# Longer links in the feed-forward chain, and the down projection's operand placed ahead of the convolution's tiles

## The chip, the cores and the metric

The kernel runs on one core of a Trainium2 chip. The metric is the device time of one execution in microseconds, given as a median of runs. The core has TensorE (PE, with its weight loads PEld), VectorE (DVE), ScalarE (ACT), GpSimd (POOL) and SyncE (SP, which issues most DMAs). Each engine works through its own list of instructions in order, and a semaphore holds an instruction back until what it needs is done.

## The reference

Two transformer blocks over 256 positions of width 2048, in float32. Each block has a mixer (attention in the first, a gated recurrence in the second) and then a feed-forward part with a convolution of width 3 over the positions. The change touches only the two feed-forward parts:

```python
# first block: causal convolution with a bias, gelu
u = causal_dwconv(h @ w_up[l], conv_w[l], conv_b[l])
gate, up = jnp.split(u, 2, axis=-1)
y = (jax.nn.gelu(gate, approximate=True) * up) @ w_down[l]
# second block: centred convolution without a bias, silu
up = dwconv3(h @ w_in, w_conv)
gate, val = jnp.split(up, 2, axis=-1)
return (jax.nn.silu(gate) * val) @ w_out
```

The inner width is 5632, so `h @ w_up` has 88 groups of 128 output features (44 of gate and 44 of up, taken alternately) and the down projection has 44 groups of 128 input features.

## The kernel before, in words

**Products.** Every float32 product is made of three: weights and activations are split into a high and a low half, and TensorE sums high by high, high by low and low by high. Weights come in *units* of 128x1024 numbers (512 KB): SP loads a unit (`ws`, L125), ACT writes its high half (`wh`, L143), DVE its low half (`wl`, L144). `Weights.ahead` splits a unit two units ahead of its use; three buffers each of `wh` and `wl` are there, so a split waits until TensorE has done with the unit three before it.

**Feed-forward stage.** The first eight groups of features are computed together (`wave`), in four PSUM banks, two groups to a bank. The other 80 are *blocks* (`block`): one group, one bank, two units, and for each unit eight matmuls of the high half (L359, 128x512) and eight of the low half (L364, 128x256). Then the down projection runs over the gated result (`v_chunk(ahl)`), four chunks of 512 columns.

**Chain.** For each group a *task* (a generator) does the work behind the product, with single instructions on ACT and DVE:

- for a block, `whole` copies half of the bank to `part` (ACT L374) and adds the other half to it (DVE L376); this add is what gives the block's bank back to TensorE
- `z` = that times the row factor R (DVE L1103); for a group of the wave this reads the bank itself and gives it back when both groups of the bank are through
- `u` = the convolution: one instruction on ACT (L1111, or L1113 in the second block), two on DVE (L1116)
- for a gate group `s` = gelu or silu of `u` (ACT L1128); for an up group `u` times `s` (DVE L1138), its high half `ah` (ACT L1141) and its low half `al` (DVE L1143), which are the down projection's operand

**What sets the order.** The kernel is recorded in the order in which Python runs, and each engine gets its instructions in that order. While matmuls are recorded, `bg.tick()` is called between them, and every fourth tick is one *step*: each waiting task runs on to its next `yield`. A unit of a block has eight ticks, so two steps; a block has four. A `yield` in a task puts what follows it one step later, and so behind whatever else is recorded meanwhile on that engine. A block's task starts when the block is recorded. The wave's eight tasks start 6 steps apart (`1 + 6 * i`).

**Banks.** There are four banks for products and two more are lent from those of the background. While the wave's tasks still hold their banks, the next block has to take the bank of a block that has just ended.

**Pools.** The tiles `z0` to `z2` (three, handed round in a list), `ah` and `al` come from one pool, placed in memory in the order of the code; `u` has four buffers and `s` two.

Of the kernel before, what the change touches and what calls it, by code (L numbers as in the profile page):

```python
# [11 lines left out]
F32 = mybir.dt.float32  # L12
F32R = mybir.dt.float32r
# [5 lines left out]
P = 128  # L19
T = 256  # L20
# [3 lines left out]
FB = DFF // P  # L24
# [146 lines left out]
def two_blocks(ctx: ExitStack, tc: tile.TileContext, a: dict, out: bass.AP, dbg=None):  # L171
    nc = tc.nc
    bg = Background()
# [39 lines left out]
    def evacuated(v):  # L213
        left = mm_use.pop(id(v))[1]
        left[0] -= 1
        if not left[0]:
            left[1].free += 1
            if left[1] is banks and lend[1]:
                lend[0] += 1
# [68 lines left out]
    def slot(name, shape=(P, KB, 2, T), dtype=F32R):  # L288
        return act_p.tile(list(shape), dtype, name=name, tag="pair")
# [60 lines left out]
    def block(src):  # L350


        ps, = mm_ps((0, 2 * T))
        for k0 in range(0, KB, 8):
            h, l = W.take()
            for j in range(8):
                k = k0 + j
                need(src, k)
                nc.tensor.matmul(ps, h[:, j, :], src.pair[:, k, :, :], start=k == 0, stop=False)  # L359
                if j % 3 < 2:  # L360
                    bg.tick()
            for j in range(8):
                k = k0 + j
                nc.tensor.matmul(ps[:, T:], l[:, j, :], src.hi[:, k, :], start=False, stop=k == KB - 1)  # L364
                if j % 4 == 3:
                    bg.tick()
        return ps

    def whole(ps):

        if ps.shape[-1] == T:
            return ps
        s = parts.tile([P, T], F32, name="part")
        nc.scalar.activation(s, ps[:, T:], AF.Copy)  # L374
        yield
        nc.vector.tensor_tensor(s, ps[:, :T], s, op=ALU.add)  # L376
        evacuated(ps)
        return s
# [317 lines left out]
    def out_chunks(src, name, yg, gb, g):  # L696

        pss = wave_t(src)
        back = Back(name, yg(), gb())
        for c in range(2):  # L700
            later(back.evac, c, pss[c])
        later(back.evac, 2, v_chunk(src, CH))
        ld = Lead(back, g)
        pss = v_chunk(src, CH, last=2, lead=ld)
        return ld, pss
# [4 lines left out]
    with first:  # L710
# [65 lines left out]
        fr, pss = boundary(None, None, G_PRE1, hhl, xT)  # L776
# [286 lines left out]
        for i in range(8):  # L1063
# [3 lines left out]
            if i in (1, 4, 5):  # L1067
# [7 lines left out]
        back, pss = out_chunks(mhl, "g_post1", lambda: ac.tile([P, 2, D], F32, name="yg", tag="bias"),  # L1075
                               lambda: slot("gb", (P, D), F32), G_PREF1)
        hp.close()
        hhl = Pair(slot("hhl"))
        fr, pss = boundary(back, pss, G_PREF1, hhl)
# [4 lines left out]
    def ffn(hhl, fr, pss, cw, cb, centred, post, g=None):  # L1084
        with ExitStack() as ph:
            fc = ph.enter_context(tc.tile_pool(name="fc", bufs=1))
            ft = ph.enter_context(tc.tile_pool(name="ft", bufs=4))
            z0 = 1 if centred else 2
            zs = [fc.tile([P, T + 32], F32, name=f"z{i}") for i in range(3)]
            for z in zs:  # L1090
                nc.vector.memset(z[:, 0:z0], 0.0)
                if centred:
                    nc.vector.memset(z[:, T + 1:T + 2], 0.0)
            ahl = Operand(fc.tile([P, FB, T], F32R, name="ah"), fc.tile([P, FB, T], F32R, name="al"))
            gated = {}
            lend[:] = 2, True

            def conv(i, ps):
                y = yield from whole(ps)
                while not zs:  # L1100
                    yield
                z = zs.pop()
                nc.vector.tensor_tensor(z[:, z0:z0 + T], y, fr.R, op=ALU.mult)  # L1103
                if y is ps:
                    evacuated(ps)
                yield
                yield
                yield
                u = ft.tile([P, T], F32, name="u")
                if cb is not None:  # L1110
                    nc.scalar.activation(u, z[:, 2:2 + T], AF.Identity, scale=cw[:, i, 2:3], bias=cb[:, i:i + 1])  # L1111
                else:
                    nc.scalar.activation(u, z[:, 2:2 + T], AF.Copy, scale=cw[:, i, 2:3])  # L1113
                yield
                for j in range(2):
                    nc.vector.scalar_tensor_tensor(u, z[:, j:j + T], cw[:, i, j:j + 1], u,  # L1116
                                                   op0=ALU.mult, op1=ALU.add)
                zs.append(z)
                return u

            def gate_task(i, ps, lag=1):
                for _ in range(lag):
                    yield
                u = yield from conv(i, ps)
                yield
                yield
                s = ft.tile([P, T], F32, name="s", bufs=2)
                nc.scalar.activation(s, u, AF.Silu if centred else AF.Gelu_apprx_tanh)  # L1128
                gated[i // 2] = s

            def up_task(i, ps, lag=1):
                for _ in range(lag):
                    yield
                u = yield from conv(i, ps)
                f = i // 2
                while f not in gated:
                    yield
                nc.vector.tensor_mul(u, gated.pop(f), u)  # L1138
                yield
                yield  # L1140
                nc.scalar.activation(ahl.hi[:, f, :], u, AF.Copy)  # L1141
                yield
                nc.vector.tensor_tensor(ahl.lo[:, f, :], u, ahl.hi[:, f, :], op=ALU.subtract)  # L1143
                ahl.ready.add(f)

            for i in range(WAVE):
                bg.add((up_task if i % 2 else gate_task)(i, pss[i], 1 + 6 * i))
            for i in range(WAVE, 2 * FB):
                bg.add((up_task if i % 2 else gate_task)(i, block(hhl)))
            back = Back(post, *yg_gb(slot("yg", (P, 3, D), F32)))  # L1150
            for c in range(3):
                later(back.evac, c, v_chunk(ahl, CH, FB))
            if g is None:
                pss = v_chunk(ahl, CH, FB, last=3)
                bg.flush()
            else:
                back = Lead(back, g)
                pss = v_chunk(ahl, CH, FB, last=2, lead=back)
            lend[:] = 0, False
        return back, pss  # L1160

    back, pss = ffn(hhl, fr, pss, convw, convb, False, "g_postf1", G_PRE2)

    with ExitStack() as ph:
# [4 lines left out]
        fr, pss = boundary(back, pss, G_PRE2, hhl)  # L1172
# [147 lines left out]
        back, pss = out_chunks(mhl, "g_post2", after_input, lambda: t[0][1], G_PREF2)  # L1320
        hp.close()
        hhl = Pair(slot("hhl"))
        fr, pss = boundary(back, pss, G_PREF2, hhl)

    back, pss = ffn(hhl, fr, pss, f2conv, None, True, "g_postf2")
# [110 lines left out]
```

## Time and profile before

| | |
|---|---|
| runs | 2578.93, 2579.96 and 2581.62 us, median 2579.96 us |
| profiled execution | 2579.38 us |
| its span, first to last instruction | 2577.6 us (1.8 us lie around it) |
| TensorE busy | 2547.7 us, 99% |
| TensorE's weight loads | 86% |
| DVE, ACT, POOL busy | 69%, 53%, 2% |
| granted TensorE clock | 0.999 |
| feed-forward stages in the trace | up projection 484 to 934 us and 1874 to 2324 us, each with 80 blocks behind its wave |

The profiled execution is the one in which the trace was taken; sums made from rows of the trace belong to its time. The span leaves out what lies before the first and behind the last instruction.

### The profile page before, as it was taken

Reading aid. Unit: us, or ns where it says so; the run is one execution under the profiler, and the core shown is the slowest. Engines: PE = TensorE matmul, PEld = TensorE weight load, DVE = VectorE, ACT = ScalarE, POOL = GpSimd, SP = SyncE. Lnnn points to the kernel's source line nnn. Section 1 sums busy time; section 2 is a strip of 40 time slices with the busy share of each in tenths; the row PEclk is TensorE's granted clock in tenths of the full one; section 3 lists DMA queues with packets and bytes.
Section 4 is the critical chain, followed back from the end, with each engine's and each line's share of the span. In section 5 each row is a group of like instructions: output and inputs, shape, how many; then the busy total and the mean of one; then the engine's idle time right before and its main releaser. Section 6 shows DMA issues by size and latency. Waiting matters only on the chain.

```text
span 2577.6 us, 38072 instructions
## 1 busy us (share of the span) xinstructions
PE 2547.7 (99%) x14400; PEld 2223.9 (86%) x14400; DVE 1771.3 (69%) x2967; ACT 1365.8 (53%) x2274; POOL 46.5 (2%) x66
## 2 busy tenths in 40 slices
PE   9999999999999999999999999999999999999998
PEld 9899988988888888889888888888988888888887
DVE  6666655687777764446777777785678877775444
ACT  5655554665555553445555555554565555554443
POOL 0000000000000000000000000000000000000000
PEclk9999999999999999999999999999999999999999
DMA  7854555556555565555544454546556555556554
GB/s 243 263 172 148 170 172 179 173 185 192 189 189 186 192 205 188 188 188 169 165 161 158 142 170 143 166 133 196 166 175 194 189 186 192 190 188 205 188 188 147
DMA packets 134229, 466.13 MB, mean 181 GB/s; under 512 B 15547, under 2 KB 20572, under 8 KB 133532
## 3 DMA queue, kind: packets, MB, share of 16 engines
q1 hardware_dynamic: 130572, 456.11, 54.9%
q10 hardware_dynamic: 2784, 2.92, 0.6%
q0 software_dynamic: 688, 4.65, 0.5%
q8 instruction: 113, 1.85, 0.3%
q14 instruction: 72, 0.59, 0.1%
HBM read 460.74 MB, written 2.88 MB: 180 GB/s over the span
## 4 chain that ended last, share of the span: by engine, by line
PE 93%; DVE 3%; ACT 2%; issue 1%; DMA 1%; POOL 0%; DVEq 0%; POOLq 0%; ACTq 0%; SPq 0%
PE mm L359 32%; PE mm L364 17%; PE mm L422 9%; PE mm L421 9%; PE mm L427 9%; PE mm L399 2%; PE mm L400 2%; PE mm L406 2%; PE bg L1248 2%; DVE wl L144 1%; ACT wh L143 1%; PE bg L421 1%; PE bg L422 1%; PE bg L427 1%; DMA ws<-in_cw 1%
## 5 line engine op out<-in xcount | busy, mean ns | idle before, releaser
L144 DVE TENSOR_TENSOR wl<-ws,wh 128x1024 fp32r<-128x1024 f32 (+1 forms) x865 | 1049.7, 1214 | 701.4 <-ACT wh L143 693.8
L143 ACT ACTIVATE wh<-ws 128x1024 fp32r<-128x1024 f32 (+1 forms) x865 | 906.5, 1049 | 743.4 <-PE mm L422 297.5
L359 PE MATMUL mm<-hhl,wh 128*128 128x512 f32 x3808 | 982.7, 396 | 3.5 <-ACT ah L1141 3.5
L359 PEld LDWEIGHTS mm<-hhl,wh 128*128 128x128 f32 x3808 | 679.3, 189 | 120.6 <-ACT ah L1141 3.8
L364 PEld LDWEIGHTS mm<-hhl,wl 128*128 128x128 f32 x3808 | 519.2, 190 | 38.1
L364 PE MATMUL mm<-hhl,wl 128*128 128x256 f32 x3808 | 530.6, 282 | 0.0
L422 PE MATMUL mm<-wh,al 128*128 128x512 f32 x684 | 269.9, 395 | 0.0
L421 PE MATMUL mm<-wh,ah 128*128 128x512 f32 x684 | 269.9, 395 | 0.0
L427 PE MATMUL mm<-wl,ah 128*128 128x512 f32 x684 | 186.7, 395 | 0.0
L427 PEld LDWEIGHTS mm<-wl,ah 128*128 128x128 f32 x684 | 128.9, 188 | 30.1
L422 PEld LDWEIGHTS mm<-wh,al 128*128 128x128 f32 x684 | 128.9, 188 | 30.0
L421 PEld LDWEIGHTS mm<-wh,ah 128*128 128x128 f32 x684 | 128.9, 188 | 30.0
L1228 ACT ACTIVATE kk<-lv 128x256 f32<-128x256 f32 x112 | 47.7, 435 | 118.1 <-DVE lv L1259 105.2
L399 PE MATMUL mm<-hhl,wh 128*128 128x256 f32 x398 | 104.8, 295 | 4.7 <-ACT wh L143 4.7
L400 PE MATMUL mm<-hhl,wh 128*128 128x256 f32 x398 | 101.0, 285 | 0.0
L376 DVE TENSOR_TENSOR part<-mm,part 128x256 f32<-128x256 f32 x238 | 99.3, 417 | 0.0
L374 ACT ACTIVATE part<-mm 128x256 f32<-128x256 f32 x238 | 87.2, 366 | 0.2
L1116 DVE SCALAR_TENSOR_TENSOR u<-z,c_convw,u 128x256 f32<-128x256 f32 x176 | 84.8, 482 | 3.1
L1116 DVE SCALAR_TENSOR_TENSOR u<-z,c_f2conv,u 128x256 f32<-128x256 f32 x176 | 84.8, 482 | 3.1
L399 PEld LDWEIGHTS mm<-hhl,wh 128*128 128x128 f32 x398 | 77.3, 194 | 5.3 <-ACT wh L143 4.7
L1248 PE MATMUL bg<-lv,kk 128*128 128x128 f32 x448 | 74.0, 288 | 5.8 <-ACT kk L1228 5.6
L1248 PEld LDWEIGHTS bg<-lv,kk 128*128 128x128 f32 x448 | 65.0, 191 | 16.1 <-ACT kk L1228 10.3
(380 smaller groups left out, 2638.0 us busy)
## 6 DMA issues: line engine op xcount, KB each, us to landing
ws<-in_wup SPq DMA_DIRECT2D x160, 512.0 KB, 3.9
ws<-in_f2in SPq DMA_DIRECT2D x160, 512.0 KB, 3.9
ws<-in_hin SPq DMA_DIRECT2D x112, 512.0 KB, 3.5
ws<-in_wdown SPq DMA_DIRECT2D x88, 512.0 KB, 3.4
ws<-in_f2out SPq DMA_DIRECT2D x88, 512.0 KB, 3.4
ws<-in_win_f SPq DMA_DIRECT2D x48, 512.0 KB, 4.0
ws<-in_hv SPq DMA_DIRECT2D x32, 512.0 KB, 3.4
ws<-in_win_vb SPq DMA_DIRECT2D x24, 384.0 KB, 3.2
```

Of the source, the lines that this page charges most:

```text
L143: self.nc.scalar.activation(h[:, c], src[:, c], AF.Copy)
L144: self.nc.vector.tensor_tensor(l[:, c], src[:, c], h[:, c], op=ALU.subtract)
L359: nc.tensor.matmul(ps, h[:, j, :], src.pair[:, k, :, :], start=k == 0, stop=False)
L364: nc.tensor.matmul(ps[:, T:], l[:, j, :], src.hi[:, k, :], start=False, stop=k == KB - 1)
L376: nc.vector.tensor_tensor(s, ps[:, :T], s, op=ALU.add)
L399: nc.tensor.matmul(pss[b], h[:, b, :], src.hi[:, k, :], start=first, stop=False, skip_group_check=True)
L400: nc.tensor.matmul(pss[b], h[:, b, :], src.lo[:, k, :], start=False, stop=False, skip_group_check=True)
L421: nc.tensor.matmul(ps, rows_of(src, k0 + j, t, 0), h[:, j, :], start=k0 + j == 0, stop=False)
L422: nc.tensor.matmul(ps, rows_of(src, k0 + j, t, 1), h[:, j, :], start=False, stop=False)
L427: nc.tensor.matmul(ps, rows_of(src, k0 + j, t, 0), l[:, j, :], start=False, stop=k0 + j == last)
L1116: nc.vector.scalar_tensor_tensor(u, z[:, j:j + T], cw[:, i, j:j + 1], u, op0=ALU.mult, op1=ALU.add)
L1248: nc.tensor.matmul(ps[:, t * P:(t + 1) * P], kk[:, t * P:(t + 1) * P], view(lv, T + t * P, [[2 * m, nb], [T + m, 2], [1, m]]), start=True, ...
```

## The change

Seven edits, all in the function `ffn`, which both blocks call:

1. `ahl` (the tiles `ah` and `al`) is allocated ahead of `z0` to `z2`, so the operand and the small tiles change places in memory.
2. In `conv`, three steps instead of one lie between the ACT part of the convolution and its DVE part.
3. In `gate_task`, three steps instead of two lie between the convolution and `s`.
4. `s` has three buffers instead of two.
5. In `up_task`, three steps instead of two lie between the product with `s` and `ah`.
6. In `up_task`, three steps instead of one lie between `ah` and `al`.
7. The wave's tasks start 10 steps apart instead of 6.

```diff
             z0 = 1 if centred else 2
+            ahl = Operand(fc.tile([P, FB, T], F32R, name="ah"), fc.tile([P, FB, T], F32R, name="al"))
             zs = [fc.tile([P, T + 32], F32, name=f"z{i}") for i in range(3)]
...
-            ahl = Operand(fc.tile([P, FB, T], F32R, name="ah"), fc.tile([P, FB, T], F32R, name="al"))
...
                     nc.scalar.activation(u, z[:, 2:2 + T], AF.Copy, scale=cw[:, i, 2:3])
                 yield
+                yield
+                yield
                 for j in range(2):
...
                 yield
                 yield
-                s = ft.tile([P, T], F32, name="s", bufs=2)
+                yield
+                s = ft.tile([P, T], F32, name="s", bufs=3)
...
                 yield
                 yield
+                yield
                 nc.scalar.activation(ahl.hi[:, f, :], u, AF.Copy)
+                yield
+                yield
                 yield
                 nc.vector.tensor_tensor(ahl.lo[:, f, :], u, ahl.hi[:, f, :], op=ALU.subtract)
...
-                bg.add((up_task if i % 2 else gate_task)(i, pss[i], 1 + 6 * i))
+                bg.add((up_task if i % 2 else gate_task)(i, pss[i], 1 + 10 * i))
```

**Place A: DVE, the fifth block of the first feed-forward stage, kernel before.** The rows are DVE's list, in order. `part<-mm` (L376) is the add that gives a block's bank back; `part_5291<-mm_5204` is that of the third block, and the fifth block's product `mm_5321` waits for it. `wl` are low halves of weights, `z1<-mm_4442` is a task of the wave.

```order
L144 TENSOR_TENSOR wl_5266<-ws_5205,wh_5265 128x1024
L1103 TENSOR_TENSOR z1_5095<-mm_4442,R_5083 128x256
L144 TENSOR_TENSOR wl_5296<-ws_5231,wh_5295 128x1024
L1143 TENSOR_TENSOR al_5101<-u_5242,ah_5100 128x256
L1116 SCALAR_TENSOR_TENSOR u_5289<-z2_5096,c_convw_120,u_5289 128x256 x2
L1138 TENSOR_TENSOR u_5289<-s_5274,u_5289 128x256
L376 TENSOR_TENSOR part_5291<-mm_5204,part_5291 128x256
```

The same stretch of DVE's list with the change, and on to the next block. Here `part_5282<-mm_5201` is the add of the third block, for which the fifth block's product `mm_5312` waits, and `part_5343<-mm_5255` that of the fourth, for which the sixth block's `mm_5370` waits.

```order
L144 TENSOR_TENSOR wl_5259<-ws_5202,wh_5258 128x1024
L1118 SCALAR_TENSOR_TENSOR u_5224<-z1_5097,c_convw_120,u_5224 128x256 x2
L144 TENSOR_TENSOR wl_5287<-ws_5228,wh_5286 128x1024
L376 TENSOR_TENSOR part_5282<-mm_5201,part_5282 128x256
L1103 TENSOR_TENSOR z1_5097<-part_5282,R_5083 128x256
L144 TENSOR_TENSOR wl_5316<-ws_5256,wh_5315 128x1024
L1118 SCALAR_TENSOR_TENSOR u_5280<-z2_5098,c_convw_120,u_5280 128x256 x2
L1141 TENSOR_TENSOR u_5280<-s_5310,u_5280 128x256
L1118 SCALAR_TENSOR_TENSOR u_5295<-z0_5096,c_convw_120,u_5295 128x256 x2
L1141 TENSOR_TENSOR u_5295<-s_5239,u_5295 128x256
L144 TENSOR_TENSOR wl_5348<-ws_5284,wh_5347 128x1024
L376 TENSOR_TENSOR part_5343<-mm_5255,part_5343 128x256
```

The third block's add moved up: nothing stands between it and the `wl` ahead of it any more. In front of the fourth block's add there now stand two convolutions, two products with `s` and two `wl`.

**Place B: DVE, the fourth block of the first stage, kernel before.** The fourth block takes the wave's first bank, `mm_4441`, which is free once its second group has gone into a `z` (L1103, last row here).

```order
L144 TENSOR_TENSOR wl_5180<-ws_5126,wh_5179 128x1024
L376 TENSOR_TENSOR part_5175<-mm_5102,part_5175 128x256
L1103 TENSOR_TENSOR z2_5096<-part_5175,R_5083 128x256
L1103 TENSOR_TENSOR z1_5095<-mm_4441,R_5083 128x256
L144 TENSOR_TENSOR wl_5208<-ws_5149,wh_5207 128x1024
```

With the change:

```order
L144 TENSOR_TENSOR wl_5178<-ws_5126,wh_5177 128x1024
L376 TENSOR_TENSOR part_5173<-mm_5102,part_5173 128x256
L1103 TENSOR_TENSOR z1_5097<-part_5173,R_5083 128x256
L1118 SCALAR_TENSOR_TENSOR u_5160<-z2_5098,c_convw_120,u_5160 128x256 x2
L144 TENSOR_TENSOR wl_5205<-ws_5149,wh_5204 128x1024
L144 TENSOR_TENSOR wl_5231<-ws_5175,wh_5230 128x1024
L376 TENSOR_TENSOR part_5226<-bg_5148,part_5226 128x256
L1103 TENSOR_TENSOR z2_5098<-part_5226,R_5083 128x256
L1103 TENSOR_TENSOR z0_5096<-mm_4441,R_5083 128x256
```

The read of `mm_4441` moved two `wl`, an add and a `z` further down, to just ahead of the fourth block.

**Place C: TensorE, the twelfth block of the first stage.** The rows are TensorE's list with what each waits for; DVE_49 and Activation_49 are the semaphores of DVE and ACT, and the first matmul of a block shows a wait for DVE when its bank may still be with DVE. Before:

```order
L359 MATMUL mm_5746<-hhl_4439,wh_5687 128x512 [waits Activation_49]
L359 MATMUL mm_5746<-hhl_4439,wh_5687 128x512 x7
L364 MATMUL mm_5746<-hhl_4439,wl_5688 128x256 [waits DVE_49]
L364 MATMUL mm_5746<-hhl_4439,wl_5688 128x256 x7
L359 MATMUL mm_5746<-hhl_4439,wh_5719 128x512 [waits Activation_49]
```

With the change:

```order
L359 MATMUL mm_5721<-hhl_4439,wh_5666 128x512 [waits DVE_49,Activation_49]
L359 MATMUL mm_5721<-hhl_4439,wh_5666 128x512 x7
L364 MATMUL mm_5721<-hhl_4439,wl_5667 128x256 [waits DVE_49]
L364 MATMUL mm_5721<-hhl_4439,wl_5667 128x256 x7
L359 MATMUL mm_5721<-hhl_4439,wh_5697 128x512 [waits Activation_49]
```

The matmuls and their order are the same; the first one of this block waits for DVE as well. Such first matmuls (DVE and ACT named) number 8 in each feed-forward stage before and 13 with the change. Apart from waits in the first fifteen blocks of the two stages TensorE's list is the same, and each engine has as many instructions of each kind as before.

## Rows read from the trace of the kernel before

**Rows 1.** The page, part 1: busy time, share of the span and instructions of each engine.

```profile
PE 2547.7 (99%) x14400; PEld 2223.9 (86%) x14400; DVE 1771.3 (69%) x2967; ACT 1365.8 (53%) x2274; POOL 46.5 (2%) x66
```

**Rows 2.** What TensorE waited for, whole run: us in total, times, longest.

```profile
PE bg L1248 <- ACT kk L1228: 5.6, 8, 1.6
...
PE mm L359 <- ACT ah L1141: 3.5, 2, 1.8
```

**Rows 3.** Busy time of each engine (instructions) in two stretches, TensorE's clock, DMA.

```profile
core 0: us, PE busy (x) PEld busy (x) DVE busy (x) ACT busy (x) POOL busy (x), PEclk, DMA share, GB/s
...
515.00:551.40 36.40, 36.39 (x208) 32.04 (x209) 32.98 (x60) 23.62 (x41) 0.00 (x0) 1.00 0.55 177
620.00:930.00 310.00, 310.00 (x1777) 272.82 (x1777) 244.09 (x392) 181.01 (x279) 0.00 (x0) 1.00 0.59 189
```

**Rows 4.** TensorE in order of time, first stage: start, us, instructions [idle before <- releaser].

```profile
501.66 2.00 PE L359 MATMUL mm<-hhl,wh 128*128 128x512 f32 x8
...
504.45 2.00 PE L359 MATMUL mm<-hhl,wh 128*128 128x512 f32 x8
506.30 1.11 PE L364 MATMUL mm<-hhl,wl 128*128 128x256 f32 x8
509.18 2.08 PE L359 MATMUL mm<-hhl,wh 128*128 128x512 f32 x8 [1.77 <-ACT ah L1141]
...
515.01 2.08 PE L359 MATMUL mm<-hhl,wh 128*128 128x512 f32 x8
...
517.89 2.00 PE L359 MATMUL mm<-hhl,wh 128*128 128x512 f32 x8
```

**Rows 5.** TensorE in order of time, second stage, same place.

```profile
1894.35 2.00 PE L359 MATMUL mm<-hhl,wh 128*128 128x512 f32 x8
...
1898.97 2.09 PE L359 MATMUL mm<-hhl,wh 128*128 128x512 f32 x8 [1.68 <-ACT ah L1141]
...
1907.69 2.00 PE L359 MATMUL mm<-hhl,wh 128*128 128x512 f32 x8
```

**Rows 6.** DVE in order of time, first stage: fourth, fifth and sixth blocks.

```profile
499.25 1.23 DVE L144 TENSOR_TENSOR wl<-ws,wh 128x1024 fp32r<-128x1024 f32 x1 [1.57 <-ACT wh L143]
...
505.76 1.23 DVE L144 TENSOR_TENSOR wl<-ws,wh 128x1024 fp32r<-128x1024 f32 x1 [0.72 <-ACT wh L143]
506.90 0.42 DVE L1143 TENSOR_TENSOR al<-u,ah 128x256 fp32r<-128x256 f32 x1
507.24 1.00 DVE L1116 SCALAR_TENSOR_TENSOR u<-z,c_convw,u 128x256 f32<-128x256 f32 x2
508.27 0.42 DVE L1138 TENSOR_TENSOR u<-s,u 128x256 f32<-128x256 f32 x1
508.62 0.42 DVE L376 TENSOR_TENSOR part<-mm,part 128x256 f32<-128x256 f32 x1
509.07 0.43 DVE L1103 TENSOR_TENSOR z<-part,R 128x256 f32<-128x256 f32 x1
509.41 1.22 DVE L144 TENSOR_TENSOR wl<-ws,wh 128x1024 fp32r<-128x1024 f32 x1
...
514.45 0.42 DVE L376 TENSOR_TENSOR part<-mm,part 128x256 f32<-128x256 f32 x1
```

**Rows 7.** ACT in order of time, same stretch.

```profile
503.60 0.42 ACT L1141 ACTIVATE ah<-u 128x256 fp32r<-128x256 f32 x1 [1.28 <-DVE u L1138]
...
506.54 1.06 ACT L143 ACTIVATE wh<-ws 128x1024 fp32r<-128x1024 f32 x1 [0.81 <-ACT wh L143]
```

**Rows 8.** TensorE's weight load at the fifth block's start.

```profile
509.15 1.68 PEld L359 LDWEIGHTS mm<-hhl,wh 128*128 128x128 f32 x8 [1.95 <-ACT ah L1141]
```

**Rows 9.** First stage, DVE: start values of the three `z` tiles.

```profile
484.68 0.08 DVE L1091 MEMSET z<- 128x2 f32 x3
```

**Rows 10.** End of the first stage: the down projection's first matmul, and the last `ah`.

```profile
934.09 0.39 PE L421 MATMUL mm<-wh,ah 128*128 128x512 f32 x1
...
945.53 0.40 ACT L1141 ACTIVATE ah<-u 128x256 fp32r<-128x256 f32 x1
```

## The prediction

> **What bounds the kernel now.** I read the page's first part, then TensorE's waits, then the stages in order of time. TensorE is busy for 99% of the span, DVE for 69%, ACT for 53% [rows 1]. A change of ACT and DVE work can therefore give back only time that TensorE stands still. In the feed-forward stages the list of waits has one entry, 3.5 us in two waits on L359, one for each stage [rows 2]; the longest entry of all (5.6 us, L1248) is in the recurrence, which the change leaves alone. In steady running nothing is lost: from 620 to 930 us TensorE is busy for 310.00 of 310.00 us and does 1777 matmuls, so a unit of 16 takes 310.00 / 1777 x 16 = 2.79 us, and DVE is busy for 244.09 us, which leaves it 21% [rows 3]. The clock is 1.00 in both stretches [rows 3], the upper of its two levels, so none is to be won back there.
>
> **What the stage starts cost.** From 504.45 to 517.89 us TensorE does four units in 13.44 us, where 4 x 2.79 = 11.16 are needed: 2.28 us lost [rows 4]. The second stage takes 1907.69 - 1894.35 = 13.34 us for the same four: 2.18 lost [rows 5]. Together 4.46 us, more than the 3.5 of the list. The rest are a second, smaller wait and slow restarts: the fifth block is due at 504.45 + 2.79 = 507.24 and starts at 509.18, 1.94 late; the sixth is due 2 x 2.79 + 0.08 later, at 514.84, and starts at 515.01, 0.17 late; and behind each stop the first eight matmuls take 2.08 instead of 2.00 us [rows 4].
>
> **What the wait is for.** The trace names `ah` as the releaser, but no block reads `ah`. The fifth block takes the third block's bank, which DVE's add (L376) gives back at 508.62 + 0.42 = 509.04 [rows 6]; TensorE's weight load follows at 509.15 [rows 8] and the matmul at 509.18, 0.14 us behind the add [rows 4]. The sixth block shows the same 0.14: add over at 514.87, start at 515.01 [rows 4, 6]. So it is a late add. Between the `wl` ahead of it and the add stand `al`, two convolution instructions and a product: from 506.90 to 508.62, 1.72 us [rows 6]. That `wl` was late as well: ACT had stood 1.28 us at an `ah` whose product was not ready [rows 7]. At the start of a stage DVE does its blocks and the wave together and is busy for 32.98 of 36.40 us [rows 3].
>
> **The change part by part.** No instruction is added or removed, so everything is a matter of place.
>
> Allocation (edit 1): the same start values without any wait, 0.08 us at 484.68 [rows 9]; I take 0 for it. If conflicts by address made every DVE instruction on `z` slower, the 21% that DVE has free in steady running would cover it [rows 3]; with that cover gone, `wl` would be late next. No row shows such an effect, and one that made them faster would not reach TensorE. The third buffer of `s` costs and gives 0 by itself: it lets ACT go on writing while an older `s` waits longer.
>
> Longer links (edits 2 to 6): they take DVE's and ACT's queues past results that are not there yet. At the end of the stage the last `ah` comes later: now at 945.53. Edits 2, 3, 5 and 6 add at most six steps up to its `al`, at two steps a unit 6 x 1.4 = 8.4 us. The down projection starts at 934.09 [rows 10] and comes to this group in its 22nd unit, at about the same 2.79 us a unit (an estimate) 59 us later. 0.
>
> The wave's spacing (edit 7) spreads its eight tasks over 70 steps instead of 42, and so holds its banks longer. With each group taking two `z`-sized instructions, two of convolution and half a product and an `al`, that thins the wave's share of DVE's work to 6/10, but the number of blocks that must ask DVE for their bank rises from 8 to 13 in a stage (place C).
>
> Now the blocks one by one, along DVE's list. Steps from start to start: `wl` 1.14 (505.76 to 506.90), a convolution pair ahead of its product 1.03, product 0.35, add to `z` 0.45, `z` 0.34; an add itself 0.42 [rows 6]. `wl` cannot start before its `wh`, and that not before TensorE's high half, so these anchors stay where the trace has them.
>
> - Fourth block (place B): its bank is now given back by the last row shown. `wl` at 499.25 [rows 6], + 1.14 + 0.45 + 0.34 puts that `z` at 501.18, over at 501.61, TensorE at 501.75. Due 501.66 [rows 4]: 0.09 late, + 0.08 for the restart = **0.17 us lost**, where nothing was lost before.
> - Fifth block (place A): the `wl` ahead of its add is set by TensorE one unit before the next anchor, at about 507.62 - 2.79 = 504.83. + 1.14 + 0.42 + 0.14 = 506.53, due 507.24: early by 0.7. **The stop of 1.94 us goes.**
> - Sixth block (place A): `wh` over at 506.54 + 1.06 = 507.60 [rows 7], `wl` at 507.62. Then, without a pause, 1.14 + 1.03 + 0.35 + 1.03 + 0.35 + 1.14 + 0.42 = 5.46: the add is over at 513.08, TensorE starts at 513.22. Due 504.45 + 3 x 2.79 = 512.82: 0.40 late, + 0.08 = **0.48 us lost**.
> - Seventh block: only an `al` stands ahead of its add; by the same steps it is 0.5 us early. The others to the fifteenth are no tighter.
>
> Left over: 0.17 + 0.48 = 0.65 a stage, 1.30 in both (the second stage's lists are the same). Gain 4.46 - 1.30 = 3.16 us. Against the profiled execution's 2579.38 (span 2577.6 and 1.8 around it) that is 2576.2. The runs' median is 0.58 higher, which would give 2576.8; I say 2576.5. The bounds: at best nothing is left over (2579.38 - 4.46 = 2574.9); at worst the two lost places, each worked out to a few tenths, cost what the stop costs today, and nothing is gained (2579.4 to 2580.0).
>
> **A rule against the change.** Of the 8 blocks in a stage that wait for DVE, two lose time and six lose nothing [rows 2, 4], so I price the late add, not the number of waits. The Trainium skill (Perfetto Trace Analysis, Optimizing Tensor Performance) advises that independent matmul groups rotate through different PSUM banks, so that emptying one bank overlaps the next group's matmuls. The change keeps the wave's banks out of that rotation for longer, so by this rule it should lose; the trace agrees with the rule in that the stops are waits for a bank, and speaks against taking the count of them as the price.
>
> **The rivals.**
>
> - *The stop only moves* (chance 0.14). The two tight places cost as much as now, for instance because ACT meets a product that is not ready, as at 503.60 [rows 7], and `wl` is late by as much again. For: 0.40 us came out of a chain of 5.46, and one more second on it gives back most of the gain. Against: the product has one step more before `ah`. 2579.4, no change.
> - *Fewer free banks* (0.08), the other side. If the loss goes with the number of blocks that wait, it grows by 13/8: 4.46 becomes 7.25, 2579.38 + 2.79 = 2582.2. If instead each of the wave's three further up groups met an add as the first does now, at 2.2 us, it would be 3 x 2 x 2.2 = 13.2 above now, 2592.6. It decides once DVE's list ahead of an add is over 5.1 us long from its `wl` on (5.46 less the 0.40 it is late) at more than the one block I found. Against: fifth and seventh blocks have 0.5 us to spare.
> - *More than the stops* (0.06). A gain of over 5.2 us needs something outside the 4.46; with TensorE busy for 36.39 of 36.40 us right behind the stops [rows 3], I see no place for it but the scatter of the runs on top of the best case.
> - My forecast, both stops mostly gone and 2575 to 2578: 0.72.
>
> **How the numbers follow.** A measurement here tells about 0.2% (5.2 us) from no change, so my likeliest case, 0.13%, counts as within it. Faster by more than that: 0.06, the third rival. Slower by more: 0.04, the dearer half of the second. Within: 0.90. The range reaches from the best case less some scatter, 2574.5, to nothing gained, 2579.9, and leaves out some 0.15.
>
> **What would show it.** Right: in the profile after, TensorE's list of waits has no 1.8 us on L359; the fifth block follows the fourth without a gap; small late starts stand at the fourth (0.1 us) and sixth block (0.4 us) in both stages, each behind an L376 or L1103; from the seventh on units come every 2.79 us. Wrong: a wait of over 1 us at any of the 13 blocks, `wl` late enough that TensorE stops between two halves of a unit, or a down projection that starts with a wait for `ah` or `al`.

## The result, and the profile after

The changed kernel takes 2564.51 us (median of 6 runs, 2563.80 to 2564.72), the kernel before 2579.47 beside it (6 runs, 2578.92 to 2581.62): 15.0 us less, ratio 0.994 with a 95% interval of 0.9930 to 0.9951. The prediction said 2576.5 and 2574.5 to 2579.9. It is wrong: the gain is nearly five times the forecast one.

The stage starts are nearly as predicted. TensorE's list of waits, the kernel after (us in total, times, longest), has no wait for `ah` on L359 any more:

```profile
PE bg L1254 <- ACT kk L1234: 5.3, 7, 1.6
...
PE mm L359 <- ACT wh L143: 0.5, 2, 0.2
```

TensorE in order of time after, the first stage's start, to be held against [rows 4] (start, us, instructions):

```profile
499.30 2.00 PE L359 MATMUL mm<-hhl,wh 128*128 128x512 f32 x8
...
502.19 2.09 PE L359 MATMUL mm<-hhl,wh 128*128 128x512 f32 x8
...
505.06 2.00 PE L359 MATMUL mm<-hhl,wh 128*128 128x512 f32 x8
...
507.85 2.00 PE L359 MATMUL mm<-hhl,wh 128*128 128x512 f32 x8
...
510.65 2.00 PE L359 MATMUL mm<-hhl,wh 128*128 128x512 f32 x8
...
513.83 2.08 PE L359 MATMUL mm<-hhl,wh 128*128 128x512 f32 x8 [0.23 <-ACT wh L143]
...
516.70 1.55 PE L359 MATMUL mm<-hhl,wh 128*128 128x512 f32 x6
```

From start to start: 2.89, 2.87, 2.79, 2.80, 3.18 and 2.87 us, 17.40 for six units that need 16.74 at 2.79. Some 0.65 us is lost, at the two places named, the fourth block, which starts at 502.19, and the sixth, at 513.83. The second stage shows the same two:

```profile
1881.36 2.00 PE L359 MATMUL mm<-hhl,wh 128*128 128x512 f32 x8
1884.26 2.06 PE L359 MATMUL mm<-hhl,wh 128*128 128x512 f32 x8
1887.10 2.00 PE L359 MATMUL mm<-hhl,wh 128*128 128x512 f32 x8
...
1892.69 2.00 PE L359 MATMUL mm<-hhl,wh 128*128 128x512 f32 x8
...
1895.88 2.08 PE L359 MATMUL mm<-hhl,wh 128*128 128x512 f32 x8 [0.24 <-ACT wh L143]
...
1898.76 2.00 PE L359 MATMUL mm<-hhl,wh 128*128 128x512 f32 x8
```

From 1881.36 to 1887.10 it is 5.74 us for two units that need 5.58, from 1892.69 to 1898.76 6.07: 0.16 + 0.49 = 0.65 lost.

DVE's rows ahead of the sixth block, after, run as the prediction's chain did, 0.6 us later by the clock of the trace:

```profile
508.24 1.23 DVE L144 TENSOR_TENSOR wl<-ws,wh 128x1024 fp32r<-128x1024 f32 x1 [0.76 <-ACT wh L143]
509.38 1.00 DVE L1118 SCALAR_TENSOR_TENSOR u<-z,c_convw,u 128x256 f32<-128x256 f32 x2
510.42 0.42 DVE L1141 TENSOR_TENSOR u<-s,u 128x256 f32<-128x256 f32 x1
510.76 1.00 DVE L1118 SCALAR_TENSOR_TENSOR u<-z,c_convw,u 128x256 f32<-128x256 f32 x2
511.79 0.43 DVE L1141 TENSOR_TENSOR u<-s,u 128x256 f32<-128x256 f32 x1
512.13 1.22 DVE L144 TENSOR_TENSOR wl<-ws,wh 128x1024 fp32r<-128x1024 f32 x1
513.27 0.42 DVE L376 TENSOR_TENSOR part<-mm,part 128x256 f32<-128x256 f32 x1
```

The add is over at 513.69, TensorE starts 0.14 later; the list of waits names a `wh`, as it named an `ah` before.

So some 12 us came from elsewhere, and the down projections show where. Busy TensorE and its instructions (x) in two stretches within them; the kernel before:

```profile
950.00:1150.00 200.00, 200.00 (x863) 1.00 0.59 189
2350.00:2550.00 200.00, 200.00 (x862) 1.00 0.59 188
```

and the kernel after:

```profile
950.00:1150.00 200.00, 200.00 (x884) 1.00 0.61 194
2350.00:2550.00 200.00, 200.00 (x884) 1.00 0.56 182
```

TensorE is busy for 200.00 of 200.00 us in both, its clock is 1.00 in both, and yet it does 2.4% more matmuls of the same shape. One instruction by its operands says it too (duration min/median/max in ns), before:

```profile
L421 PE MATMUL mm<-wh,ah x684: 390/393/404, 934.1 to 2559.5; 128*128 128x512 f32 x171
...
L421 PE MATMUL mm<-wh,mh x88: 389/389/497, 338.3 to 424.8; 128*128 128x512 f32 x88
```

and after:

```profile
L421 PE MATMUL mm<-wh,ah x684: 389/389/396, 932.9 to 2544.8; 128*128 128x512 f32 x171
```

By the median the same matmul was slower on `ah` than on the attention's `mh` before the change; after it both take 389. The means would have hidden it, because some of the matmuls on `mh` take up to 497 ns. Groups of instructions before (busy us, mean ns of one):

```profile
L421 PE MATMUL mm<-wh,ah 128*128 128x512 f32 x684 | 269.9, 395 | 0.0
...
L421 PE MATMUL mm<-wh,mh 128*128 128x512 f32 x88 | 34.9, 397 | 0.0
```

From the starts in the traces I worked out the time from one matmul's start to the next within a unit of the down projection: eight matmuls on `wh`, then four on `wl`. In these products `wh` and `wl` are the moving operand, the one that runs through TensorE, and `ah` and `al` (in turn on `wh`, `ah` alone on `wl`) the stationary one, which the weight load brings in before. The rows are means over 73 to 76 units from 950 to 1160 us; rows for the experiments stand here too.

```
                 eight on wh                               four on wl          unit, ns
before           232 232 233 233 232 233 232 232           233 232 232 233     2788.6
after            227 227 227 227 227 227 227 227           227 227 227 227     2720.0
gap64            231 236 231 236 231 236 231 236           231 236 231 236     2800.0
al_only          235 231 238 229 228 233 235 231           231 236 228 233     2786.7
al_grouped       227 227 227 233 241 232 231 233           231 227 227 227     2760.0
wl128            232 233 231 227 227 227 227 227           234 224 238 229     2753.3
```

A unit is 68.6 ns shorter; 2112 matmuls are 176 units: 12.1 us.

### The profile page after: what moved, and what is told of

It reads as the page before. It is cut to its first block, busy times and chain, and to the rows that moved or that the text cites. A ratio compares the mean times of both kernels' runs of the same rounds, so it can differ in the third digit from the quotient of the medians.

```text
span 2562.7 us, 38160 instructions
## 1 busy us (share of the span) xinstructions
PE 2536.6 (99%) x14400; PEld 2222.3 (87%) x14400; DVE 1783.4 (70%) x2967; ACT 1356.4 (53%) x2274; POOL 46.5 (2%) x66
## 4 chain that ended last, share of the span: by engine, by line
PE 93%; DVE 3%; ACT 2%; issue 1%; DMA 1%; POOL 0%; DVEq 0%; POOLq 0%; ACTq 0%; SPq 0%
PE mm L359 33%; PE mm L364 17%; PE mm L422 9%; PE mm L421 9%; PE mm L427 9%; PE mm L399 2%; PE mm L400 2%; PE mm L406 2%; PE bg L1254 2%; ACT wh L143 1%; DVE wl L144 1%; DMA ws<-in_cw 1%; PE bg L421 1%; PE bg L422 1%; PE bg L427 1%
## 5 line engine op out<-in xcount | busy, mean ns | idle before, releaser
L359 PE MATMUL mm<-hhl,wh 128*128 128x512 f32 x3808 | 982.6, 396 | 0.5 <-ACT wh L143 0.5
L359 PEld LDWEIGHTS mm<-hhl,wh 128*128 128x128 f32 x3808 | 679.2, 189 | 117.6 <-ACT wh L143 0.8
L422 PE MATMUL mm<-wh,al 128*128 128x512 f32 x684 | 266.1, 389 | 0.0
L421 PE MATMUL mm<-wh,ah 128*128 128x512 f32 x684 | 266.1, 389 | 0.0
L421 PEld LDWEIGHTS mm<-wh,ah 128*128 128x128 f32 x684 | 128.4, 188 | 26.6
L422 PEld LDWEIGHTS mm<-wh,al 128*128 128x128 f32 x684 | 128.4, 188 | 26.6
L376 DVE TENSOR_TENSOR part<-mm,part 128x256 f32<-128x256 f32 x238 | 99.4, 417 | 0.0
```

The source lines that it names most:

```text
L421: nc.tensor.matmul(ps, rows_of(src, k0 + j, t, 0), h[:, j, :], start=k0 + j == 0, stop=False)
L422: nc.tensor.matmul(ps, rows_of(src, k0 + j, t, 1), h[:, j, :], start=False, stop=False)
```

## The experiments

Edit 1 moves `ah` and `al` by three tiles of (256 + 32) x 4 = 1152 bytes, 3456 = 13 x 256 + 128. In the memory map of the built program `ws`, `wh`, `wl`, `hhl`, `mh` and `ml` all start at 128 modulo 256. Before, `ah` and `al` alone of these products' operands started at 0; after, they start at 128 as well. My theory: the place of `ah` and `al` sets the pace of the down projections. The rival: the longer links took ACT and DVE out of the down projections' way, and the place does nothing. A `gap` below is a tile that nothing uses. Each run's ratio is taken against the kernel before on the same chip; a difference from the changed kernel is one of medians from different sessions.

**One part alone.** `place_only` is the kernel before with edit 1:

```diff
+            ahl = Operand(fc.tile([P, FB, T], F32R, name="ah"), fc.tile([P, FB, T], F32R, name="al"))
             zs = [fc.tile([P, T + 32], F32, name=f"z{i}") for i in range(3)]
...
-            ahl = Operand(fc.tile([P, FB, T], F32R, name="ah"), fc.tile([P, FB, T], F32R, name="al"))
```

> The kernel before with ah and al allocated ahead of the three z tiles, and nothing else. Theory 'place' (the down projection's matmuls run faster because their stationary operand starts at another address): the two stops at the stage starts stay as they were (loss 2.28 and 2.18 us), and the down projections' 2112 matmuls go from about 232 to about 227 ns each, 2112 x 5.7 ns = 12.0 us less: about 2567.5 us, and the mean of one L421 matmul falls from 395 to about 389 ns. Theory 'chain' (the longer links of the feed-forward's chain made the down projection faster, and the place does nothing): 2579.5 us and 395 ns. The prediction on record took 0 for this edit: 2579.5 us.

Measured 2566.83 us against 2578.92: 12.1 us less, ratio 0.9953 (0.9938 to 0.9968). Its waits still hold the two stops, and its down projections run at the new pace:

```profile
PE mm L359 <- ACT ah L1141: 3.5, 2, 1.8
```

```profile
950.00:1150.00 200.00, 200.00 (x884) 1.00 0.59 193
```

`chain_only` is the changed kernel with that line moved back:

```diff
-            ahl = Operand(fc.tile([P, FB, T], F32R, name="ah"), fc.tile([P, FB, T], F32R, name="al"))
             zs = [fc.tile([P, T + 32], F32, name=f"z{i}") for i in range(3)]
...
+            ahl = Operand(fc.tile([P, FB, T], F32R, name="ah"), fc.tile([P, FB, T], F32R, name="al"))
```

> The changed kernel with ah and al back behind the z tiles: the longer links, the wave 10 apart and the third s alone. Theory 'place': the stage starts as in the changed kernel (loss 0.65 us in each), the down projections as before (L421 at 395 ns): 2579.5 - 3.2 = 2576.3 us, which is also what the prediction on record gives. Theory 'chain': all of the gain, 2564.5 us, L421 at 389 ns.

Measured 2576.09 us, 2.8 less than before, ratio 0.9986 (0.9976 to 0.9996). The stops are gone and the pace is the old one:

```profile
PE mm L359 <- ACT wh L143: 0.5, 2, 0.2
```

```profile
950.00:1150.00 200.00, 200.00 (x863) 1.00 0.58 189
```

12.1 + 2.8 = 14.9 of the 15.0 us. The rival is out, and the two parts add up.

**Order or address.** `shift128`, in the changed kernel:

```diff
+            fc.tile([P, 32], F32, name="gap")
             ahl = Operand(fc.tile([P, FB, T], F32R, name="ah"), fc.tile([P, FB, T], F32R, name="al"))
```

> The changed kernel with an unused tile of 128 bytes in each partition allocated just ahead of ah and al, which still stand ahead of the z tiles: their start goes from 128 to 0 modulo 256. If it is the start address modulo 256 that matters: the down projections as before, L421 at about 395 ns, some 2576.3 us. If it is the order of the tiles (ah and al lying next to what stands ahead of them, not behind the z tiles): 2564.5 us, L421 at 389 ns.

Measured 2576.09 us: 128 unused bytes bring the loss back. L421 on `ah`, by the groups of instructions (busy, mean ns of one):

```profile
L421 PE MATMUL mm<-wh,ah 128*128 128x512 f32 x684 | 269.8, 395 | 0.0
```

`z_first_gap`, in the changed kernel:

```diff
+            zs = [fc.tile([P, T + 32], F32, name=f"z{i}") for i in range(3)]
+            fc.tile([P, 160], F32, name="gap")
             ahl = Operand(fc.tile([P, FB, T], F32R, name="ah"), fc.tile([P, FB, T], F32R, name="al"))
-            zs = [fc.tile([P, T + 32], F32, name=f"z{i}") for i in range(3)]
```

> The changed kernel with ah and al behind the z tiles again, but with an unused tile of 640 bytes in each partition between, so that ah and al start at 128 modulo 256 as in the changed kernel. If it is the start address modulo 256 that matters: 2564.5 us, L421 at 389 ns. If it is the order of the tiles: about 2576.3 us, L421 at about 395 ns.

Measured 2564.02 us; with the `z` tiles ahead of them again, `ah` and `al` cost nothing as long as they start at 128:

```profile
L421 PE MATMUL mm<-wh,ah 128*128 128x512 f32 x684 | 266.1, 389 | 0.0
```

So it is the address, not the order.

**Address or distance.** `pad160` moves everything by 128 bytes:

```diff
-    small.tile([P, 8], F32, name="pad", bufs=1)
+    small.tile([P, 40], F32, name="pad", bufs=1)
```

> The changed kernel with the unused tile at the head of the memory 160 bytes long instead of 32, so that every operand of TensorE, weights and activations, moves by 128 bytes: all start at 0 modulo 256, and none differs from another. Theory 'distance' (what counts is how far the stationary operand lies from the moving one, modulo 256): as the changed kernel, 2564.5 us, L421 on ah at 389 ns. Theory 'address' (a stationary operand that starts at 0 modulo 256 is slow wherever the moving one lies): the down projections slow, 12 us, L421 on ah at 395 ns, and the other products that were fast (the attention's, L399 to L406 and L421 to L427 on hhl, in the hundreds of matmuls each) slower too: 2576.5 us at least, and up to 2600 us if the block products' 3856 matmuls of 512 columns lose 5.7 ns each as well.

Measured 2563.84 us: every operand at 0 is as good as every one at 128. `pad160_gap128` has `shift128`'s line besides:

> The same with another 128 bytes ahead of ah and al: the stationary operand of the down projections at 128 modulo 256 as in the changed kernel, the moving one at 0. Theory 'distance': slow again, 2576.3 us, L421 on ah at 395 ns. Theory 'address': the down projections fast, L421 on ah at 389 ns, with the other products as in the run with every operand at 0.

Measured 2575.23 us, with `ah` at the very 128 modulo 256 that was fast, but `wh` and `wl` at 0:

```profile
L421 PE MATMUL mm<-wh,ah 128*128 128x512 f32 x684 | 269.8, 395 | 0.0
```

What counts is the distance between the stationary and the moving operand. `gap64` has 64 bytes for `shift128`'s 128:

```diff
+            fc.tile([P, 16], F32, name="gap")
```

> The changed kernel with an unused tile of 64 bytes ahead of ah and al: the start at 192 modulo 256, the moving operand at 128. If any difference slows: 2576.3 us, L421 on ah at 395 ns. If the loss grows with the difference up to 128: about 2570.5 us, 392 ns. If only a difference of 128 bytes slows (both still begin in the same half of 256 bytes): 2564.5 us, 389 ns.

Measured 2578.04 us: a difference of 64 bytes slows too, and costs more than 128 (13.5 against 11.6 us over the changed kernel's 2564.51). Its steps are another pattern, 231 and 236 by turns. The pattern repeats whatever ACT and DVE do meanwhile: each of the 74 units averaged above takes 2800 ns. That speaks against a clash with the reads and writes of other engines. `gap256` has 256 bytes there:

```diff
+            fc.tile([P, 64], F32, name="gap")
```

> The changed kernel with an unused tile of 256 bytes ahead of ah and al: still 128 modulo 256 like the moving operand, but another address modulo 512, 1024 and 2048. If the distance counts modulo 256: 2564.5 us, L421 on ah at 389 ns. If it counts modulo more than that: slow, about 2576 us, 395 ns.

Measured 2563.62 us. A distance of 256 is as good as none, and 64 and 128 are slow: as far as these three tell, the distance counts modulo 256. Below, two operands are *in line* when their starts lie a multiple of 256 bytes apart, and *off the line* otherwise.

**Whose operand pays.** `al_only` puts the 128 bytes between `ah` and `al`:

```diff
+            ah = fc.tile([P, FB, T], F32R, name="ah")
+            fc.tile([P, 32], F32, name="gap")
-            ahl = Operand(fc.tile([P, FB, T], F32R, name="ah"), fc.tile([P, FB, T], F32R, name="al"))
+            ahl = Operand(ah, fc.tile([P, FB, T], F32R, name="al"))
```

> The changed kernel with 128 bytes between ah and al: ah at 128 modulo 256, al at 0. If each matmul pays for its own stationary operand: a third of the down projections' 2112 matmuls have al, so 12.0 / 3 = 4.0 us more than the changed kernel, 2568.5 us. If one slow operand sets the pace of all of them: 2576.3 us. If al alone does nothing: 2564.5 us.

Measured 2575.20 us. I had put the loss of a third first; nearly the whole loss is there (a unit of 2786.7 ns for 2788.6 before), with only one matmul in three off the line. `wl128` moves the low halves of the weights alone (its lines count two higher):

```diff
+    ctx.enter_context(tc.tile_pool(name="ga", bufs=1)).tile([P, 32], F32, name="ga")
     wl_p = ctx.enter_context(tc.tile_pool(name="wl", bufs=3))
+    ctx.enter_context(tc.tile_pool(name="gb2", bufs=1)).tile([P, 32], F32, name="gb2")
```

> The changed kernel with 128 bytes ahead of the low halves of the weights (wl) and 128 behind, so that wl alone starts at 0 modulo 256 and everything else keeps its 128. In the down projections wl is the moving operand of one matmul in three (L427); in the block products it is the stationary operand of the 256-column matmuls (L364). If a matmul pays for its own pair of operands: 704 x 5.7 ns = 4.0 us in L427, 2568.5 us, and up to 3856 x 5.7 ns = 22 us more if L364 pays as well, 2590 us. If one operand off the line sets the pace of all, as the run with al alone had it: 12 us in the down projections, 2576.3 us, and more with L364. If distance 128 suits a 256-column matmul better than 0: less than these.

Measured 2575.70 us. A unit of the down projection takes 2753.3 ns, 33.3 more than in the changed kernel (176 x 33.3 ns = 5.9 us), and a unit of a block 2806.7 for 2793.3 (the program has 480 of them, two fewer than I had counted: 6.4 us). That makes 12.3 us; measured are 11.2 over 2564.51. Neither "its own pair" (4.0 us) nor "the pace of all" (12 us) fits the 5.9. The steps listed above say why: the four matmuls on `wl` are uneven, the next three on `wh` still take 232, 233 and 231 ns although their own operands are in line, and then the pace is 227 again. With `ah` and `al` in turn it never comes so far: in `al_only` the four matmuls on `wl`, all in line, take 231, 236, 228 and 233 ns, so three is no fixed number. That made a new theory, "settles", which `al_grouped` tests: `al_only` with the four matmuls on `ah` ahead of the four on `al`.

```diff
-        for j in range(n):
-            need(src, k0 + j)
-            for t, ps in enumerate(pss):
-                nc.tensor.matmul(ps, rows_of(src, k0 + j, t, 0), h[:, j, :], start=k0 + j == 0, stop=False)
-                nc.tensor.matmul(ps, rows_of(src, k0 + j, t, 1), h[:, j, :], start=False, stop=False)
-                bg.tick()
+        for half in range(2):
+            for j in range(n):
+                need(src, k0 + j)
+                for t, ps in enumerate(pss):
+                    nc.tensor.matmul(ps, rows_of(src, k0 + j, t, half), h[:, j, :],
+                                     start=k0 + j == 0 and not half, stop=False)
+                bg.tick()
```

> The run with al alone off the line (al at 0, ah, wh and wl at 128 modulo 256), with the eight matmuls of a unit on wh in another order: the four with ah first, then the four with al, where they alternated. Theory 'settles' (a matmul off the line, and some three in line behind it, are slow, then the pace is flat again, as the run with wl moved had it): per unit of twelve about 33 ns less than with al alternating, 176 units, 5.9 us: 2575.2 - 5.9 = 2569.3 us. Theory 'sets the pace of all': 2575.2 us as before.

Measured 2570.66 us, 4.5 less than with `al` in turn. TensorE in order of time shows one unit, `ah` 0.91 us, `al` 0.94, `wl` 0.91:

```profile
1001.37 1.08 PE L422 MATMUL mm<-wh,ah 128*128 128x512 f32 x4
1002.28 1.10 PE L422 MATMUL mm<-wh,al 128*128 128x512 f32 x4
1003.22 1.07 PE L428 MATMUL mm<-wl,ah 128*128 128x512 f32 x4
1004.13 1.08 PE L422 MATMUL mm<-wh,ah 128*128 128x512 f32 x4
```

The steps from the last `ah` on are 233, 241, 232, 231, 233 and 231 ns, then 227 again: "settles" holds, with a unit 26.7 ns shorter than with `al` in turn where 33 were expected. Behind the four on `al` only one matmul in line, the first on `wl`, is slow (231 ns). The last matmul on `ah` is slow already (233 ns), although its operands are in line like those of the three before it; what differs is the next one's weights, `al`. In `wl128` the last matmul ahead of `wl` still takes 227 ns, and there the next one's weights are `ah`, in line. Both would fit a clash between the moving operand of one matmul and the weight load for the next, which no run tests by itself. The control, `grouped`, is the changed kernel with this order and no gap:

> The changed kernel with that order alone and no gap (control): all operands in line, 2564.5 us, L421 at 389 ns, by either theory.

Measured 2564.43 us: the order alone does nothing.

**The block products.** `hhl128` moves the moving operand of the blocks (its lines count one higher):

```diff
     x = act_p.tile([P, 2, D], F32, name="x")
+    act_p.tile([P, 32], F32, name="gap")
...
         hhl = Pair(slot("hhl"))
+        act_p.tile([P, 32], F32, name="gap2")
```

> The changed kernel with the tile of the activations' pairs (hhl) alone moved by 128 bytes, to 0 modulo 256, and the distance of every other pair of operands kept. The block products (L359 and L364, hhl moving, weights stationary) then have their operands 128 apart. If the rule holds for them as for the down projections: L359 goes from 230.1 to about 232.4 ns from start to start, 3856 x 2.3 ns = 8.9 us, some 2573.5 us, and more where L364 pays too. If it is a matter of the down projections alone: 2564.5 us.

Measured 2571.21 us, 6.7 more than the changed kernel. The rule holds for the blocks too, a unit taking 2810.1 for 2793.3 ns. Not all of the 480 units are moved: in the memory map the recurrence's blocks read another tile, which keeps its distance (their units take 2884 ns by the median with and without the gap). The attention and the two feed-forward parts have 368, and 368 x 16.8 = 6.2 us. My expectation was wrong in saying that every other pair keeps its distance: the moved tile is also the stationary operand of products in attention and recurrence (L422 and L423). The loss lies in the 512-column matmuls, 20.8 ns a unit; the eight of 256 columns take 4.0 ns less. TensorE from 620 to 930 us does 1768 instructions where [rows 3] has 1777:

```profile
620.00:930.00 310.00, 310.00 (x1768) 1.00 0.61 187
```

Even in line a block's unit is not flat: its first five matmuls of 512 columns take 233, 236, 228, 233 and 231 ns, then three 227, and of those of 256 columns two take 113 and 119, the other six 120. Two kernels tried to win from that. `flip` mirrors the second unit of each block:

```diff
+            for high in (True, False) if k0 == 0 else (False, True):
+                for j in range(8):
...
+                    if high:
+                        nc.tensor.matmul(ps, h[:, j, :], src.pair[:, k, :, :], start=k == 0, stop=k == KB - 1)
...
+                    else:
+                        nc.tensor.matmul(ps[:, T:], l[:, j, :], src.hi[:, k, :], start=False, stop=False)
```

> The changed kernel with the two units of each block product in mirrored order: eight matmuls of 512 columns and eight of 256 in the first, eight of 256 and eight of 512 in the second, so that 512-column matmuls follow 256-column ones half as often. In the changed kernel the first five 512-column matmuls of a unit take 25 ns more in all than the flat 227 ns of the last three. If that loss belongs to the switch: half of it goes, 482 / 2 x 25 ns = 6.0 us, about 2558.5 us. If it belongs to the unit: 2564.5 us. If the low halves of the weights, now wanted earlier in every second unit, come late: above 2564.5 us with TensorE waiting for wl.

Measured 2563.12 us. Its profiled execution took 12574.97 us, with matmuls of blocks over three times as long as usual, so no row is read from it. `flip_again` is the same kernel:

> The kernel with mirrored units once more, for a usable profile: 2563.1 us as before. If the loss behind the switch was halved and something else took it back, the second unit's matmuls (256 columns first) show it: 120 ns for all sixteen 256-column matmuls where the first one or two of each eight took 113 and 119.

Measured 2562.91 us. The mirrored order does what was expected: sixteen matmuls of 512 columns in a row are uneven five times, not ten, and a block takes 5566.7 ns for 2 x 2793.3 = 5586.6, 240 x 20 ns = 4.8 us less. It is given back in waits for weights, the list of TensorE's waits:

```profile
PE bg L1255 <- ACT kk L1235: 5.9, 10, 1.6
PE mm L843 <- DVE wl L144: 4.9, 7, 1.0
...
PE mm L361 <- ACT wh L143: 2.4, 2, 1.2
PE mm L842 <- ACT wh L143: 1.2, 1, 1.2
```

In the changed kernel these four are 5.3, 3.5, 0.5 and 0.7: 4.4 us more. What is left, 1.6 us on the medians, cannot be told from no change. `alternate` takes 512 and 256 columns in turn:

```diff
                 nc.tensor.matmul(ps, h[:, j, :], src.pair[:, k, :, :], start=k == 0, stop=False)
-                if j % 3 < 2:
-                    bg.tick()
-            for j in range(8):
-                k = k0 + j
                 nc.tensor.matmul(ps[:, T:], l[:, j, :], src.hi[:, k, :], start=False, stop=k == KB - 1)
-                if j % 4 == 3:
-                    bg.tick()
+                bg.tick()
```

> The changed kernel with the block products' matmuls of 512 and of 256 columns in turn instead of eight and eight. If only matmuls of 256 columns behind one another are slow (the first behind a 512-column one took 113 ns, the later ones 120) and those of 512 columns settle: up to 8 x 6 ns + 25 ns = 73 ns per unit less, 35 us, 2530 us. If every switch disturbs (233 + 114 to 120 ns a pair, or 236 + 120): between 2562 and 2570 us. If wl, now wanted at once, comes late: above that, with TensorE waiting for wl.

Measured 2575.28 us. In the profiled execution every switch disturbs, and the price in my expectation was too low: from 700 to 930 us a pair takes 236.7 + 116.7 = 353.3 ns, a unit 2826.7 for 2793.3, 480 x 33.4 = 16.0 us. On 2564.51 that is 2580.5, near this execution's 2582.04. TensorE also waits there for banks (4.5 us on L359, for DVE's `part` and `z`), but not for `wl` in a block. The other seven runs lie between 2567.52 and 2583.12 us, six of them below 2580.5, so the full price cannot hold in all of them; what makes them lie so far apart stays open. No version beat the changed kernel by more than can be measured.

## Why the prediction was wrong, and where it was right

- **"Allocation (edit 1) … I take 0 for it"** is the step that failed. It asked what conflicts by address would do to DVE's instructions on `z`, and not to TensorE's reads of the operand that edit 1 moves as well. In its place the runs show 12.1 us (`place_only`), a matter of 128 bytes (`shift128`, `z_first_gap`). The other terms together came out within 0.4 us (`chain_only`).
- **What bounds the kernel.** "In steady running nothing is lost" was read off 310.00 busy of 310.00 us [rows 3]. A TensorE that is always busy need not be at its best pace: before and after, the down projections are 100% busy at a clock of 1.00, 2.4% apart. From this came "can give back only time that TensorE stands still", and the chance of 0.06 for a larger gain, put down to scatter. The row that speaks against it was in the trace of before, L421 on `ah` at 393 ns beside 389 on `mh`, and I did not compare one line by its operands; by the means (395 and 397) it would not have shown.
- The Trainium skill (SBUF — State Buffer, "SBUF: two separate sides") says that on the engines' side only the port pair that VectorE and GpSimd share causes contention and that TensorE's port waits for nobody; the section behind it ("A bandwidth-pool intuition that's wrong (but worth ruling out)") gives the weight load a second, independent read port. By that, edit 1 would be worth 0. The measurement decides: TensorE's pace depends on how the addresses of its two operands lie to each other, 232 against 227 ns.
- **The stage starts** were right. Forecast: 4.46 us lost go down to 0.17 + 0.48 a stage; measured: 0.18 + 0.47 in the first stage and 0.16 + 0.49 in the second. `chain_only` gains 2.8 us for 3.16 forecast, 2576.09 for 2576.5. The chain of DVE's rows, from `wl` to add, takes 513.69 - 508.24 = 5.45 us for 5.46.
- **The end of the stage** cost nothing, as said: the last `ah` comes at 946.88, 1.4 us later than in [rows 10].
- **The rivals.** The stop did not move, and 13 blocks that ask DVE for their bank cost no more than 8 did: 0.5 us of waits on L359 for 3.5 [rows 2]. The Trainium skill (Perfetto Trace Analysis, "Optimizing Tensor Performance") advises that matmul groups rotate through different PSUM banks; keeping the wave's banks out of that rotation for longer shows no price here beyond the 0.65 us a stage. "More than the stops" was right in its sign and had no mechanism.

Open is what in the memory or in TensorE makes 256 bytes the unit, why 64 bytes off cost more than 128, and why the pace takes several matmuls to settle. No run measured this outside the kernel.

## What to carry to other kernels

Before pricing an allocation at nothing, list the start addresses of every pair of operands of TensorE and compare the same matmul line by its operands: a few ns between groups of equal shape is time that no list of waits shows. Compare medians, or the time from start to start: here the means would have pointed the other way. Here the cure was 128 bytes, and a tile of 64 or 128 bytes allocated ahead of the operand undid it. Where an edit moves several things, give every moved thing its own sentence, the one that is not the edit's purpose too.

## What the runs showed of the hardware

- In the down projections, where matmuls of 512 columns follow one another, the time from start to start is 227 ns when stationary and moving operand start a multiple of 256 bytes apart (as far as was tried), 232 on average at 128 bytes, 233 at 64.
- The disturbance outlasts its cause by a number of matmuls that differs: one in `al_grouped`, three in `wl128`, at least four in `al_only`. In every block five of 512 columns behind a run of 256-column ones are uneven.
- Matmuls of 256 columns, operands in line, take 113 ns for the first, 119 for the second and 120 for the later ones of eight. At a distance of 128 bytes they are no slower in sum in `hhl128` (948.5 for 952.5 ns), but are in `wl128` (962.5).
